# Branch, output and gate/up projections planned by the first stage's list scheduler, with pools opened by phase and shared PSUM

## The chip, the core and the metric

One NeuronCore of a Trainium2 chip runs one decoder layer. The metric is the device time of one execution in microseconds (us). Engines: PE is TensorE (PEld its weight loads), DVE is VectorE, ACT is ScalarE, POOL is GpSimd, SP is the queue that issues most DMAs; ACT issues some DMAs from its own queue. Each engine works through its instructions in the order in which they were recorded, and an instruction that waits holds up all behind it.

## What is computed

```python
S = D_MODEL = 1024; FFN_HIDDEN = 2816
xn = rms_norm(x, norm1_g); proj = xn @ w_in          # q k v | q f i g | two gates
o_sb = stick_breaking_attention(q, k, v)              # 8 heads of 64
o_hg = hgrn2_mixer(...)                               # 4 heads of 128
mixed = sigmoid(gate_sb) * (o_sb @ w_branch[:512]) + sigmoid(gate_hg) * (o_hg @ w_branch[512:])
h = x + mixed @ w_out
hn = rms_norm(h, norm2_g)
out = h + (silu(hn @ w_gate) * (hn @ w_up)) @ w_down
```

All in float32. The matrix products are made of three products of split operands: a value is hi (rounded) plus lo (the rest), and hi·hi + lo·hi + hi·lo are summed in PSUM.

## The kernel before

Everything is transposed (features on partitions, time along the free axis, two halves `h` of 512 columns). It runs in five stages.

1. **First stage** (input projections, attention, HGRN2; all records have line 182, where the plan issues them). `Plan` collects operations with an engine, a duration and a rank; `issue` is a list scheduler that replays them on a model clock and records, on each free engine, the ready operation of highest rank and longest remaining way, once the buffers (`ring`s of a given size) that it needs are free. The gate projections, units `G`, come last; their raw values go to DRAM (`sig_d`) by ACT's queue.
2. **Branch projection** (`pj`, `z` banks; lines 305 to 307): eight blocks `i` of w_branch; attention and HGRN2 outputs are loaded from DRAM (`o_d`) and split. For each block two gates are loaded (`s0`, `s1`), multiplied by the row norm `rr1` on POOL (line 808), put through a sigmoid on ACT (809), and multiplied and added on DVE (816 to 818) into the mixed rows `mx` (hi `ah`, lo `al`).
3. **Output projection** (lines 305 to 307 again, bank `pj`): eight blocks of w_out in the order 0, 4, 1, 5, ..., two halves each. Each result gets x added (862, `xx`), is stored to `h_d` (863, ACT's queue), scaled by the norm's weight (865), squared and summed into `rr` (872, 873), and combined and split into seven Winograd operands `fop` (884 to 889, 848, 849).
4. **Gate/up** (line 919, banks `f`): a Strassen-Winograd form of one level. For each of 11 passes `p`, `left` loads two blocks of w_gate (or w_up) and makes seven split operands (`a_ops`: 902, 903, 905, 910, and 237/238 for the split), and `winograd` makes seven products of 12 matmuls each in three banks x, y, z. After product 1 ACT copies x to `p1` (970 in the first call, 979 later); DVE adds y and p1 after product 6 (976 in the first call, 981 later), before product 7 may go on into the same y bank; further sums are at 986 to 991. A pass is one gate call and one up call, 168 matmuls. `channel_sums` (line 927 on) makes the second norm inside the first call. `down_sums` (945, 955, 958) prepares sums of w_down and writes them to DRAM for stage 5; the results of a pass go to `act_d`.
5. **Down projection** (line 1068), seven products over 11 operand pairs each, accumulated in four banks.

Stages 2 to 5 are written as straight code and put in order by the framework's own scheduler. Stages 1 to 3 have three, two and three PSUM banks called pj, z and ms; stages 4 and 5 rotate through all eight as `f`.

The first `winograd` call is written like this, with `begin` being `channel_sums`:

```python
prod(x, a[1], fop[1], True)
nc.scalar.copy(p1, x)
prod(z, a[5], fop[5], True)
prod(y, a[6], fop[6], True, range(3))
prod(x, a[2], fop[2], False)
prod(y, a[6], fop[6], True, (3,))
begin()
nc.vector.tensor_tensor(c[:, 1], y, p1, op=ALU.add)
prod(y, a[7], fop[7], False)
```

Of the kernel before, what the change touches and what calls it, by code (L numbers as in the profile page):

```python
# [10 lines left out]
F32 = mybir.dt.float32  # L11
# [55 lines left out]
class Buf(View):  # L67
    def __init__(self, ring, make):
        super().__init__(self, lambda t: t)
        self.ring, self.make, self.tile = ring, make, None  # L70
        self.writers, self.readers, self.left, self.held = [], [], 0, False


class Plan:
# [6 lines left out]

    FROM = {"P": 0.2, "D": 2.0}
    TO = {"P": 0.35}

    def __init__(self):
        self.ops, self.caps, self.land = [], {}, {}

# [3 lines left out]
    def op(self, eng, us, calls, rank=0, after=(), part=False, holds=(), lat=None, land=None):  # L91
# [27 lines left out]
        self.ops.append((eng, us, calls, rank, deps, after, bufs, lat))  # L119
        if land:  # L120
            self.land[i] = land
        return i

    def issue(self):
# [18 lines left out]

        way = [0.0] * n
        for i in range(n - 1, -1, -1):
            way[i] = ops[i][1] + max(
                [way[j] + delay(i, j, data) for j, data in succ[i] if ops[j][3] >= 0 or data],
                default=0.0)
        order = lambda i: (-ops[i][3], -way[i], i)
# [9 lines left out]
        while done < n:  # L159
# [6 lines left out]
            for e in engines:  # L166
                while free[e] <= t:
                    for i in ready[e]:
                        need = [b for b in ops[i][6] if b.ring and not b.held]
                        if early[i] <= t and all(  # L170
# [5 lines left out]
                    ready[e].remove(i)  # L176
                    _, us, calls, rank, deps, after, bufs, lat = ops[i]
# [25 lines left out]
def hybrid_block(ctx: ExitStack, tc, xT, wi, wb, wo, wg, wu, wd, vec, outT):  # L203
# [145 lines left out]
    tmpp = st1.enter_context(tc.tile_pool(name="tmpp", bufs=1, reuse_waits="tile"))  # L349
# [12 lines left out]
    where = {tag: (pool, cap) for pool, tags in RINGS.items() for tag, cap in tags.items()}  # L362

    def new(tag, shape=(P, HALF), dt=F32):
        pool, cap = where[tag]
        plan.ring(tag, cap)
        return Buf(tag, lambda: pool.tile(list(shape), dt, tag=tag, bufs=cap, name=tag))
# [4 lines left out]
    def A(fn, *args, n=HALF, aps=0, rank=0, ps=False, part=False, holds=(), **kw):  # L372
        us = (0.05 if ps else 0.093) + n / 1200 + 0.0935 * aps
        return plan.op("A", us, [(fn, args, kw)], rank, part=part, holds=holds)
# [23 lines left out]

    act, tt = nc.scalar.activation, nc.vector.tensor_tensor
    stt, ts = nc.vector.scalar_tensor_tensor, nc.vector.tensor_scalar  # L400

    def rstd(dst, ss, n, rank=0):
        A(act, dst, ss, AF.Ln, ps=True, aps=1, bias=eps_t, scale=1.0 / n, rank=rank)
        A(act, dst, dst, AF.Exp, scale=-0.5, rank=rank)
# [35 lines left out]
    def load(dst, src, kb):  # L440
        last_load[0] = L(dst, src, kb, rank=1, after=(last_load[0],))
# [81 lines left out]
    def take(nm, u, h, ps):  # L523
# [17 lines left out]
        elif nm == "G":  # L541
            x = new("tmp")
            A(nc.scalar.copy, x, ps, ps=True)
            plan.op("A", 0.1, [(nc.scalar.dma_start, (sig_d[u][:, hs(h)], x), {})], lat=2.5)
# [55 lines left out]
    def values(j, last):  # L600
# [12 lines left out]
        for e in range(2):  # L613
            own, oth = slice(64 * e, 64 * e + 64), slice(64 - 64 * e, 128 - 64 * e)
            for sb in range(4):
# [29 lines left out]
                L(o_d[j][own, sb * 256:(sb + 1) * 256], ot[own], 64)  # L645
        return last

    def hgrn(hd, last):
# [5 lines left out]
        for h in range(2):  # L654
# [89 lines left out]
            L(o_d[4 + hd][:, hs(h)], o, 256)  # L744
# [15 lines left out]
    for i, (nm, u) in enumerate(fill):  # L760
# [7 lines left out]
        elif i > 1:  # L768
            w = take_w(COL[nm] + u)
# [6 lines left out]
            if nm == "hg":  # L776
                ends = [f(u, e) for f, e in zip((scores, values, hgrn), ends)]
    with tc.manual_schedule():
        plan.issue()
    c1.close()  # L780
    st1.close()
    st2 = ExitStack()
    op_ = st2.enter_context(tc.tile_pool(name="opool", bufs=1, side="right", reuse_waits="tile"))
    mt = st2.enter_context(tc.tile_pool(name="mt", bufs=2, side="right", reuse_waits="tile"))
    oo = []
    for k in range(KT):
        t = mt.tile([P, S], F32, tag="ld", bufs=4, name="o32")
        nc.sync.dma_start(t, o_d[k])
        hi = op_.tile([P, S], F32R, name=f"oh{k}")
        lo = op_.tile([P, S], F32R, name=f"ol{k}")  # L790
        nc.scalar.copy(hi, t)
        nc.vector.tensor_tensor(lo, t, hi.bitcast(F32), op=ALU.subtract)
        oo.append((hi, lo))
    xst.close()
    mst = ExitStack()
    mx = a_set(mst.enter_context(tc.tile_pool(name="mxp", bufs=1, reuse_waits="tile")))
    wq = [get_w(wb[0])]
    for i in range(KT):
        w = wq.pop(0)
        if i + 1 < KT:  # L800
            wq.append(get_w(wb[i + 1]))
        s0 = mt.tile([P, S], F32, tag="s0", bufs=2, name="s0")
        s1 = mt.tile([P, S], F32, tag="s1", bufs=2, name="s1")
        nc.sync.dma_start(s0, sig_d[i])
        nc.sync.dma_start(s1, sig_d[KT + i])
        for s in (s0, s1):
            for h in range(2):
                nc.gpsimd.tensor_tensor(s[:, hs(h)], s[:, hs(h)], rr1[h], op=ALU.mult)  # L808
            nc.scalar.activation(s, s, AF.Sigmoid)
        for h in range(2):  # L810
            y0, y1 = pj(), pz()
            mm3(y0, w, full[:4], oo, h)
            mm3(y1, w, full[4:], oo, h)
            t0 = mt.tile([P, HALF], F32, tag="t0", name="t0")
            t1 = mt.tile([P, HALF], F32, tag="t1", name="t1")
            nc.vector.tensor_tensor(t0, y0, s0[:, hs(h)], op=ALU.mult)
            nc.vector.tensor_tensor(t1, y1, s1[:, hs(h)], op=ALU.mult)
            nc.vector.tensor_tensor(t0, t0, t1, op=ALU.add)
# [332 lines left out]
```

## Time and profile before

| | us |
|---|---|
| median of 3 runs | 1529.68 (1528.2 to 1530.11) |
| the profiled execution | 1531.17 |
| its span, first to last instruction | 1529.4 |
| PE busy in the span | 1500.8 |

The profile is of one execution; the time around its span is 1531.17 - 1529.4 = 1.77 us. Busy time counts instructions that run, so an engine's idle time is the span less its busy time. In timelines a row has start, duration, engine, line, operation, output and input, and in brackets the idle time before it and what ended that. In rows of waits the numbers are the total, how often, and the longest.

### The profile page before, as it was taken

The page shows a single profiled execution, that of the slowest core. Times are in us where ns is not written, and L with a number is a line of the kernel's source. Part 1 is how long each engine was busy: PE and PEld are TensorE (multiplying, and loading weights), DVE is VectorE, ACT ScalarE, POOL GpSimd, SP SyncE. Part 2 cuts the span into 40 slices and gives each one's busy share as a digit, 9 for nine tenths or more (in the row PEclk, how much of TensorE's full clock was granted, in tenths as well). Part 3 has the DMA queues.
Part 4 walks back from the last instruction along what each step waited for, and adds up shares of the span by engine and source line. Part 5 has one row for each costly group of instructions (what it writes and reads, how often), then busy time and mean ns, then how long its engine had stood idle before and what let it go on. Part 6 is the DMA issues. An engine that isn't in the chain of part 4 may idle for free.

```text
span 1529.4 us, 20448 instructions
## 1 busy us (share of the span) xinstructions
PE 1500.8 (98%) x7213; PEld 1241.2 (81%) x7213; DVE 1179.9 (77%) x2060; ACT 799.1 (52%) x1503; POOL 160.5 (10%) x189
## 2 busy tenths in 40 slices
PE   8999999999999999999999979999999999999999
PEld 6788888888888888888878868888888888878887
DVE  8899779987898777965557789888887777475553
ACT  7866768578858879444333352333333333254442
POOL 4210111111111110114420000000000000000000
PEclk9999999999999999999999999999999999999999
DMA  5111211111111121145434436666633333687672
GB/s 180 42 39 42 83 32 43 47 44 59 41 51 54 59 68 49 52 143 208 139 111 150 140 128 223 221 214 220 221 110 110 111 110 117 245 302 223 191 220 93
DMA packets 78407, 188.53 MB, mean 123 GB/s; under 512 B 9056, under 2 KB 11104, under 8 KB 76896
## 3 DMA queue, kind: packets, MB, share of 16 engines
q1 hardware_dynamic: 68368, 168.34, 33.7%
q10 hardware_dynamic: 9936, 18.88, 3.3%
q8 instruction: 57, 0.93, 0.3%
q14 instruction: 46, 0.38, 0.1%
HBM read 131.61 MB, written 55.57 MB: 122 GB/s over the span
## 4 chain that ended last, share of the span: by engine, by line
PE 72%; DVE 12%; DMA 6%; ACT 4%; issue 4%; POOL 2%; SPq 0%; POOLq 0%; ACTq 0%; DVEq 0%
PE pj L182 24%; PE f L919 20%; PE f L1068 12%; PE ms L182 8%; PE z L182 2%; DMA w<-wu 2%; PE pj L306 2%; PE pj L305 2%; PE pj L307 2%; DVE ol L238 2%; DMA s<-sig_d 1%; ACT aa L182 1%; DMA rb<-act_d 1%; POOL s L808 1%; DMA h_d<-xx 1%
## 5 line engine op out<-in xcount | busy, mean ns | idle before, releaser
L182 PE MATMUL pj<-ah,oh 128*128 128x512 f32 x704 | 286.6, 407 | 1.9 <-POOL oh L182 1.9
L182 PE MATMUL pj<-ah,ol 128*128 128x512 f32 x704 | 276.4, 393 | 1.1 <-DVE ol L182 1.0
L182 PE MATMUL pj<-al,oh 128*128 128x512 f32 x704 | 276.0, 392 | 0.0
L919 PE MATMUL f<-fh,oh 128*128 128x512 f32 x616 | 241.4, 392 | 11.2 <-ACT p L970 7.1
L919 PE MATMUL f<-fl,oh 128*128 128x512 f32 x616 | 240.5, 390 | 0.0
L919 PE MATMUL f<-fh,ol 128*128 128x512 f32 x616 | 240.4, 390 | 0.0
L237 ACT CAST oh<-w 128x512 fp32r<-128x512 f32 x168 | 102.5, 620 | 186.6 <-PE f L919 132.2
L182 PEld LDWEIGHTS pj<-ah,ol 128*128 128x128 f32 x704 | 132.6, 188 | 31.8 <-DVE ol L182 2.4
L182 PEld LDWEIGHTS pj<-ah,oh 128*128 128x128 f32 x704 | 133.0, 189 | 25.4 <-POOL oh L182 2.9
L182 PEld LDWEIGHTS pj<-al,oh 128*128 128x128 f32 x704 | 133.0, 189 | 22.7 <-issue 0.5
L919 PEld LDWEIGHTS f<-fh,oh 128*128 128x128 f32 x616 | 116.1, 189 | 38.4 <-ACT p L970 7.6
L238 DVE TENSOR_TENSOR ol<-w,oh 128x512 fp32r<-128x512 f32 x168 | 115.1, 690 | 35.5 <-ACT oh L237 35.2
L919 PEld LDWEIGHTS f<-fh,ol 128*128 128x128 f32 x616 | 116.1, 188 | 24.5
L919 PEld LDWEIGHTS f<-fl,oh 128*128 128x128 f32 x616 | 116.2, 189 | 23.8
L182 DVE TENSOR_TENSOR_SCAN aa<-aa,ww 128x128 f32<-128x128 f32 (+3 forms) x96 | 92.2, 975 | 33.4 <-ACT aa L182 23.9
L1068 PE MATMUL f<-bh,ah 128*128 128x512 f32 x296 | 114.9, 390 | 1.1 <-ACT acc L1094 1.1
L1068 PE MATMUL f<-bl,ah 128*128 128x512 f32 x296 | 115.4, 390 | 0.5 <-DVE bl L238 0.5
L1068 PE MATMUL f<-bh,al 128*128 128x512 f32 x296 | 115.2, 389 | 0.0
L182 POOL TENSOR_SCALAR oh<-w 128x512 fp32r<-128x512 f32 x84 | 71.1, 846 | 394.2 <-PE pj L182 355.2
L238 DVE TENSOR_TENSOR al<-ra,ah 128x512 fp32r<-128x512 f32 x73 | 50.4, 690 | 76.8 <-ACT ah L237 76.8
L237 ACT CAST ah<-ra 128x512 fp32r<-128x512 f32 x73 | 45.6, 625 | 104.0 <-PE f L1068 92.9
L182 ACT ACTIVATE aa<-aa 128x512 f32<-128x512 f32 (+3 forms) x128 | 69.1, 553 | 4.9 <-DVE aa L182 4.0
(270 smaller groups left out, 2971.2 us busy)
## 6 DMA issues: line engine op xcount, KB each, us to landing
w<-wi SPq DMA_DIRECT2D x42, 512.0 KB, 3.6
rb<-act_d SPq DMA_DIRECT2D x73, 256.0 KB, 4.4
w<-wg SPq DMA_DIRECT2D x22, 512.0 KB, 4.1
w<-wu SPq DMA_DIRECT2D x22, 512.0 KB, 3.7
w<-wd SPq DMA_DIRECT2D x22, 512.0 KB, 7.0
wd_d<-ds SPq DMA_DIRECT2D x44, 256.0 KB, 5.6
ra<-wd_d SPq DMA_DIRECT2D x44, 256.0 KB, 4.1
act_d<-c SPq DMA_DIRECT2D x10, 1024.0 KB, 3.9
```

Source lines behind the costliest of these rows:

```text
L182: fn(*[a.real() if isinstance(a, View) else a for a in args], **{k: v.real() if isinstance(v, View) else v for k, v in kw.items()})
L237: pin(nc.scalar.copy(hi, src))
L238: pin(nc.vector.tensor_tensor(lo, src, hi.bitcast(F32), op=ALU.subtract))
L305: nc.tensor.matmul(out, hi[:, ws], a[ka][0][:, hs(h)], start=first and i == 0, stop=False)
L306: nc.tensor.matmul(out, hi[:, ws], a[ka][1][:, hs(h)], start=False, stop=False)
L307: nc.tensor.matmul(out, lo[:, ws], a[ka][0][:, hs(h)], start=False, stop=last and i == n - 1)
L808: nc.gpsimd.tensor_tensor(s[:, hs(h)], s[:, hs(h)], rr1[h], op=ALU.mult)
L919: nc.tensor.matmul(out, a[i][:, ws], bl[k][j], start=start and k == 0 and i + j == 0, stop=k == 3 and i == 1, skip_group_check=True)
L1068: nc.tensor.matmul(bank[d], l[:, ws], r, start=start and i == 0, stop=p == NP - 1 and i == 2, skip_group_check=True)
```

## The change

Stages 2 to 4 become operations of the same `Plan`, with durations, and one `issue` call records stages 1 to 4. PE's order of matmuls is fixed by a chain (`after=(turn,)`): from the last projection of the first stage on, each group of three waits in the plan for the one before. All other engines take what the list scheduler gives them; stage comes before rank. Pools of later stages are opened when the first of their tiles is recorded, and a tile of phase 2 to 5 is held back in the plan until all operations of the parts named in `BEFORE` are recorded. The gate/up stage uses the banks pj (x), ms (y) and z (z) in rings of 3, 3 and 2 instead of eight `f` banks; `psum2` is opened for stage 5 alone. The gates are multiplied by the row norm on DVE instead of POOL. Results go to `act_d` in eight transfers of 256 KB a pass instead of one of 1024 KB and four of 256 KB. The sum t7 is made in place instead of in a temporary, and all temporaries of stage 3 but one come from the ring `f` of 56. Stages 1 and 5 keep their code.

```diff
+    STAGE = {"s1": 0, "G": 0, "wb": 1, "wo": 1, "ffn": 1}
+    BEFORE = {0: (), 2: ("s1",), 3: ("s1", "G"), 4: ("s1", "G", "wb"), 5: ("s1", "G", "wb", "wo")}
...
-        order = lambda i: (-ops[i][3], -way[i], i)
+        order = lambda i: (stage[i], -ops[i][3], -way[i], i)
...
-                        if early[i] <= t and all(
+                        if early[i] <= t and not any(
+                                left[p] for p in self.BEFORE[phase[i]]) and all(
                                 slots[b.ring] >= sum(c.ring == b.ring for c in need)
                                 for b in need):
...
+    LATER = {
+        ("mt", 2): dict(ld=(4, "ld"), s0=(2, "s0"), s1=(2, "s1"), t0=(2, "t0"), t1=(2, "t1")),
+        ("op", 2): dict(oo=(16, "o")),
+        ("wot", 3): dict(y=(4, "y")),
+        ("mx", 3): dict(mx=(16, "mx")),
+        ("s2p", 4): dict(s2=(2, "s2")),
+        ("fp", 4): dict(f=(56, "f"), rr=(2, "rr")),
+        ("preB", 5): dict(w2=(2, "w"), ds=(4, "ds"), bs=(4, "bs")),
+        ("wA", 5): dict(wA=(2, "w"), ohA=(4, "oh"), olA=(4, "ol")),
+        ("fa", 5): dict(g=(4, "g"), c=(4, "c"), p1=(2, "p1")),
+    }
...
-        for s in (s0, s1):
-            for h in range(2):
-                nc.gpsimd.tensor_tensor(s[:, hs(h)], s[:, hs(h)], rr1[h], op=ALU.mult)
...
+            t = new(ring, (P, S))
+            L(t, sig[j], 512)
+            for h in range(2):
+                V(tt, t[:, hs(h)], t[:, hs(h)], rr[h], op=ALU.mult)
+            A(act, t, t, AF.Sigmoid, n=S + (0 if i or ss else TABLE))
...
-                        t7, t6 = tmp("t7"), blk[0, 0]
-                        nc.vector.tensor_tensor(t7, y, blk[0, 1], op=ALU.subtract)
...
+                    t7, t6 = blk[0, 1], blk[0, 0]
+                    V(tt, t7, y, t7, op=ALU.subtract)
...
+    def prod(out, a, p, start, ks=range(4)):
...
+            turn = plan.op("P", 0.69, [
+                (nc.tensor.matmul, (out, a[p][i][:, ws], fop[p][k][j]),
+                 dict(start=start and k == 0 and i + j == 0, stop=k == 3 and i == 1,
+                      skip_group_check=True)) for i, j in ((0, 0), (0, 1), (1, 0))], after=(turn,))
...
+        x, y, z, p1 = new("pj"), new("ms"), new("z"), new("p1")
+        prod(x, a, 1, True)
+        A(nc.scalar.copy, p1, x, ps=True)
+        if first:
+            prod(z, a, 5, True)
+            prod(x, a, 2, False, (0, 1))
+            prod(y, a, 6, True)
+            channel_sums()
+            V(tt, c[1], y, p1, op=ALU.add)
+            prod(y, a, 7, False)
+            prod(x, a, 2, False, (2, 3))
+        else:
+            prod(y, a, 6, True)
+            V(tt, c[1], y, p1, op=ALU.add)
+            prod(z, a, 5, True)
+            prod(y, a, 7, False)
+            prod(x, a, 2, False)
...
+        for b, t in enumerate((*c, n7, n6, n5, n4)):
+            dst = actd[p][:, b * HALF:(b + 1) * HALF]
+            store_a(dst, t) if p == NP - 1 else L(dst, t, 256, part=True)
...
+    sta.close()
+    preB = pools["preB"]
     psum_st.close()
```

In the recorded order the first stage stays as it was on every engine until its last operations beside the G units, and PE makes the same 6919 matmuls and transposes. The first place where the order differs in weight is ACT's, at the border of the output projection and gate/up. Before (f, yy, t and s are operands of `fop` and of the weight sums, w weights, `parts` the split norm, `p_9238` the copy p1, xx the rows of h):

```order
L863 DMA h_d_152<-xx 128x512
L872 ACTIVATE sq<-xx 128x512
L237 CAST oh<-w_9198 128x512
L927 CAST parts<-rr_8385 128x512
L848 CAST fh<-yy 128x512
L848 CAST fh<-t_9125 128x512
L237 CAST oh<-w_9160 128x512
L848 CAST fh<-yy 128x512
L237 CAST oh<-s_9206 128x512
L848 CAST fh<-yy 128x512
L237 CAST oh<-w_9162 128x512
L970 COPY p_9238<-f 128x512
```

Now, on the same engine at the same place (every planned record has line 194; `bs` is the split norm, y the scaled rows of the last block, `p_9185` the copy p1):

```order
L194 CAST bs<-rr 128x512
L194 CAST oh<-w 128x512
L194 ACTIVATE f<-f 128x512
L194 DMA h_d_152<-f 128x512
L194 CAST f<-y 128x512
L194 COPY p_9185<-pj 128x512
L194 CAST bs<-rr 128x512
L194 CAST oh<-w 128x512
L194 CAST f<-y 128x512 x2
```

The copy p1 stood eight rows behind the split of the norm's second half (`parts<-rr_8385`); it now stands one row ahead of it, behind the square and one cast of the last block.

The second place is DVE's, between the last sum of a pass (z into c) and the first sum of the next gate call (y and p1 into g), at the border of passes 0 and 1. Before:

```order
L991 TENSOR_TENSOR c_9375<-f_9415,c_9375 128x512
L238 TENSOR_TENSOR ol_9546<-w32_9527,oh_9545 128x512
L1013 TENSOR_TENSOR c_9375<-c_9375,g_9197 128x512
L945 TENSOR_TENSOR ds_9982<-w32_9978,ds_9981 128x512
L1016 TENSOR_TENSOR bs_9512<-c_9375 128x512
L238 TENSOR_TENSOR ol_9401<-w32_9376,oh_9400 128x512
L1020 TENSOR_TENSOR bs_9513<-bs_9512,c_9375 128x512
L910 TENSOR_TENSOR w32_9376<-w32_9376,s2_9384 128x512
L1016 TENSOR_TENSOR bs_9514<-c_9375,bs_9513 128x512
L1016 TENSOR_TENSOR bs_9515<-c_9375,bs_9513 128x512
L238 TENSOR_TENSOR ol_9405<-w32_9378,oh_9404 128x512
L981 TENSOR_TENSOR g_9524<-f_9563,p1_9565 128x512
```

Now:

```order
L194 TENSOR_TENSOR c_9412<-z_9405,c_9412 128x512
L194 TENSOR_TENSOR ol_9537<-s2_9509,oh_9529 128x512
L194 TENSOR_TENSOR c_9412<-c_9412,g_9261 128x512
L194 TENSOR_TENSOR c_9501<-c_9501,g_9387 128x512
L194 TENSOR_TENSOR bs_9552<-c_9456,c_9412 128x512
L194 TENSOR_TENSOR ds_9562<-ds_9487,w_9444 128x512
L194 TENSOR_TENSOR ol_9568<-w_9236,oh_9554 128x512
L194 TENSOR_TENSOR bs_9572<-bs_9552,c_9481 128x512
L194 TENSOR_TENSOR ds_9577<-w_9458,ds_9487 128x512
L194 TENSOR_TENSOR g_9585<-ms_9548,p1_9560 128x512
```

Ten instructions stood between the two sums; now eight do, and two of the four `bs` sums follow behind.

The third is DVE's order while PE works on the last G units (o are the split rows of `o_d`, s_7546 the first gate, ol the low halves of weights); before, the two `ol<-w` stood ahead of all `o` rows. Now:

```order
L194 TENSOR_TENSOR o<-ld,o 128x1024 x4
L194 TENSOR_TENSOR s_7546<-s_7546,rr_0_95 128x512
L194 TENSOR_TENSOR s_7546<-s_7546,rr_1_96 128x512
L194 TENSOR_TENSOR ol<-w,oh 128x512
L194 TENSOR_TENSOR o<-ld,o 128x1024
L194 TENSOR_TENSOR ol<-w,oh 128x512
L194 TENSOR_TENSOR s_7600<-s_7600,rr_0_95 128x512
```

The last `ol<-w` is the second half of the last G weight, which PE needs before stage 2; it now stands behind a gate and five rows of `o_d` that come by DMA.

## Rows read from the trace of the kernel before

**Rows 1.** Page, part 1: busy time, share of the span, instructions.
```profile
PE 1500.8 (98%) x7213; PEld 1241.2 (81%) x7213; DVE 1179.9 (77%) x2060; ACT 799.1 (52%) x1503; POOL 160.5 (10%) x189
```
**Rows 2.** Busy time of each engine by stretch; the header names the columns.
```profile
core 0: us, PE busy (x) PEld busy (x) DVE busy (x) ACT busy (x) POOL busy (x), PEclk, DMA share, GB/s
...
673.00:702.00 29.00, 29.00 (x129) 24.00 (x128) 14.45 (x15) 16.14 (x20) 6.22 (x6) 1.00 0.85 306
702.00:790.80 88.80, 87.39 (x385) 72.01 (x385) 52.00 (x73) 32.42 (x45) 38.32 (x29) 1.00 0.36 123
790.80:877.80 87.00, 87.00 (x385) 72.05 (x384) 62.53 (x105) 32.05 (x56) 0.00 (x0) 1.00 0.43 138
877.80:1313.20 435.40, 424.22 (x1853) 348.52 (x1853) 361.64 (x582) 144.67 (x239) 0.00 (x0) 0.99 0.47 160
1313.20:1529.40 216.20, 210.87 (x925) 172.86 (x923) 120.22 (x190) 85.59 (x152) 0.00 (x0) 1.00 0.68 221
```
**Rows 3.** PE's waits: total us, times, longest.
```profile
PE f L919 <- ACT p L970: 7.1, 1, 7.1
PE f L919 <- DVE g L981: 3.0, 5, 0.8
...
PE z L305 <- DVE t L817: 1.4, 1, 1.4
...
PE f L919 <- DVE g L986: 1.0, 1, 1.0
```
**Rows 4.** Timeline of PE, DVE and ACT behind the output projection, each engine by itself.
```profile
885.12 0.39 PE L919 MATMUL f<-fh,ol 128*128 128x512 f32 x1
892.64 0.79 PE L919 MATMUL f<-fh,oh 128*128 128x512 f32 x1 [7.14 <-ACT p L970]
...
885.43 0.69 DVE L884 TENSOR_TENSOR t<-yy 128x512 f32<-128x512 f32 x1 [2.89 <-DMA h_d<-xx]
886.04 0.68 DVE L873 TENSOR_TENSOR rr<-rr,sq 128x512 f32<-128x512 f32 x1
...
886.76 0.62 ACT L927 CAST parts<-rr 128x512 fp32r<-128x512 f32 x1 [3.20 <-DVE rr L873]
...
892.01 0.58 ACT L970 COPY p<-f 128x512 f32<-128x512 f32 x1
```
**Rows 5.** Busy time by stretch, as in Rows 2, just behind that gap.
```profile
892.64:897.10 4.46, 4.46 (x11) 3.49 (x12) 4.46 (x9) 1.14 (x2) 0.00 (x0) 0.50 0.42 118
```
**Rows 6.** PE at the end of the branch projection; POOL's group of gate products.
```profile
786.15 0.39 PE L307 MATMUL pj<-oh,ol 128*128 128x512 f32 x1
787.95 0.50 PE L305 MATMUL z<-oh,oh 128*128 128x512 f32 x1 [1.41 <-DVE t L817]
...
L808 POOL TENSOR_TENSOR s<-s,rr 128x512 f32<-128x512 f32 x32 | 43.3, 1380 | 59.5 <-DMA s<-sig_d 59.5
```
**Rows 7.** DVE around the border of passes 0 and 1; one pass by stretch.
```profile
923.26 0.69 DVE L902 TENSOR_TENSOR w<-w,w 128x512 f32<-128x512 f32 x1 [1.30 <-DMA w<-wu]
...
929.53 0.68 DVE L991 TENSOR_TENSOR c<-f,c 128x512 f32<-128x512 f32 x1
...
936.15 0.68 DVE L981 TENSOR_TENSOR g<-f,p 128x512 f32<-128x512 f32 x1
...
900.00:938.60 38.60, 36.84 (x161) 29.66 (x160) 35.58 (x59) 16.50 (x26) 0.00 (x0) 1.00 0.60 209
```
**Rows 8.** DMA issues: queue, count, KB each, median us from issue to landing.
```profile
w<-wd SPq DMA_DIRECT2D x22, 512.0 KB, 7.0
wd_d<-ds SPq DMA_DIRECT2D x44, 256.0 KB, 5.6
...
h_d<-xx ACTq DMA_DIRECT2D x16, 256.0 KB, 3.5
```
**Rows 9.** ACT's splits of the rows of o_d in the G tail.
```profile
689.88 1.05 ACT L791 CAST oh<-o 128x1024 fp32r<-128x1024 f32 x1 [0.69 <-DMA o<-o_d]
```
**Rows 10.** DVE's last sum of gate/up.
```profile
1313.43 0.69 DVE L991 TENSOR_TENSOR c<-f,c 128x512 f32<-128x512 f32 x1 [1.30 <-PE f L919]
```

More of the change, by code (lines that the diff above doesn't have):

```diff
@@ L361, in hybrid_block @@
     }
[L362 to L367, printed above, removed]
+    where = {tag: (pool, cap, tag, 0) for pool, tags in RINGS.items() for tag, cap in tags.items()}
+    pools, now = {}, [0]
+    st2, fst, mst, sta = ExitStack(), ExitStack(), ExitStack(), ExitStack()
+    LATER = {
[9 more added lines that the diff above has]
+    }
@@ L369, in fixed, with new, make, A @@
+    def new(ring, shape=(P, HALF), dt=F32):
+        pool, cap, tag, phase = where[ring]
+        plan.ring(ring, cap)
+        def make():
+            open_pools(phase)
+            return (pools[pool] if phase else pool).tile(list(shape), dt, tag=tag, bufs=cap, name=tag)
+        return Buf(ring, make, phase)
     def fixed(tile):
         return Buf(None, lambda: tile)
-    def A(fn, *args, n=HALF, aps=0, rank=0, ps=False, part=False, holds=(), **kw):
+    def A(fn, *args, n=HALF, aps=0, rank=0, ps=False, part=False, holds=(), after=(), **kw):
@@ L776, in hybrid_block, with full_split, get_w @@
             if nm == "hg":
+                plan.part = "s1"
                 ends = [f(u, e) for f, e in zip((scores, values, hgrn), ends)]
+    def full_split(src, rings=("oh", "ol"), rank=0):
+        hi, lo = new(rings[0], dt=F32R), new(rings[1], dt=F32R)
+        A(nc.scalar.copy, hi, src, rank=rank)
+        V(tt, lo, src, hi.bitcast(F32), op=ALU.subtract, rank=rank)
+        return hi, lo
+    def get_w(src):
+        t = new("w", (P, 1024))
+        load(t, src, 512, rank=0)
+        return [full_split(t[:, 512 * i:512 * i + 512]) for i in range(2)]
@@ new lines, in hybrid_block, with products @@
+    TABLE = 1536
+    plan.part = "wb"
+    turn = last_fill[0]
+    oo = []
+    for k in range(KT):
+        t = new("ld", (P, S))
+        L(t, od[k], 512)
+        hi, lo = new("oo", (P, S), F32R), new("oo", (P, S), F32R)
+        A(nc.scalar.copy, hi, t, n=S)
+        V(tt, lo, t, hi.bitcast(F32), op=ALU.subtract, n=S)
+        oo.append((hi, lo))
+    def products(out, w, a, ks, h, k0=0, last=True):
+        nonlocal turn
+        for n, k in enumerate(ks):
+            hi, lo = w[(k0 + n) // 4]
+            ws = slice((k0 + n) % 4 * P, ((k0 + n) % 4 + 1) * P)
+            turn = M(1536, [(out, hi[:, ws], a[k][0][:, hs(h)], n == 0, False),
+                            (out, hi[:, ws], a[k][1][:, hs(h)], False, False),
+                            (out, lo[:, ws], a[k][0][:, hs(h)], False, last and n == len(ks) - 1)],
+                     after=(turn,))
@@ L778, in hybrid_block @@
     with tc.manual_schedule():
         plan.issue()
[L780 to L793, printed above, removed]
```

415 lines of the change are left out of this document (201 added, 214 removed).

## The prediction

> **What bounds the kernel now.** I read the page's shares first: PE is busy for 1500.8 of the span of 1529.4 us [rows 1], so the kernel ends when PE has made its products, and a change that adds or removes no product can move the time only through the 28.6 us in which PE stands still, through PE's clock, or by making new idle time. The table by stage says where those 28.6 us lie [rows 2]. While PE works on the last G units it has no gap (29.00 of 29.00); in the branch projection it stands still for 88.80 - 87.39 = 1.41 us, in the output projection not at all, in gate/up for 435.40 - 424.22 = 11.18 us, in the down projection for 216.20 - 210.87 = 5.33 us. The rest lies in the first stage. The first stage keeps its order and the last keeps its code, so what the change can win is in the 12.6 us of the middle.
>
> The waits name them [rows 3]: one of 7.1 us for ACT's copy p1, five of about 0.6 us (3.0) for DVE's sum that frees the y bank, one of 1.0 us for a sum of z, and one of 1.4 us in the branch projection for DVE's t. Together 12.5 us. The reader should also see what is not there: no wait for a weight and none for x. PE's pace where nothing stops it is the output projection's 87.00 / 385 = 0.226 us a matmul [rows 2].
>
> A wait costs a little more than the row names. In the branch projection the matmul before starts at 786.15 and the next at 787.95 [rows 6]: 1.80 - 0.226 = 1.57 us where 1.41 are named, 0.16 more. Eight such waits make 1.3 us. The long one costs something else too. Behind it, PE ran at a granted clock of 0.50, the level of 1.2 GHz, and eleven matmuls took 4.46 us [rows 5]; at 0.226 they take 2.49, so 1.97 us were lost. PE had stood still for 7.14 us just before [rows 4]. All that this stretch of the program can give back is 12.5 + 1.3 + 1.97 = **15.8 us**.
>
> **The change, part by part.**
>
> *The border of output projection and gate/up.* PE stopped because ACT had not copied x into p1 (892.01) [rows 4]. Followed back: ACT's copy stood eight rows behind `parts<-rr`, which started at 886.76 after a wait of 3.20 us for DVE's addition into rr (886.04). That addition was late because the instruction ahead of it on DVE, t7, had itself waited 2.89 us for a store of xx to `h_d` to land. t7 is a new temporary in a ring of seven, and the ring's oldest tile was still being stored. So a store held DVE, DVE held ACT, ACT held PE. The change makes t7 in place, which takes away the store's wait, and puts p1 ahead of the second `parts` row and of the casts. Either alone would shorten the chain. I count the whole wait as gone: 7.1 + 0.16 + 1.97 = 9.2 us.
>
> What is late next there? DVE. Between PE's last product of the output projection and the first sum of y and p1 it has the last xx sum and fifteen more instructions. One takes 0.61 us from start to start where DVE does not wait (885.43 to 886.04) [rows 4], so the y sum starts 16 × 0.61 = 9.8 us after the projection's end and ends 0.69 later, at about 10.5. PE makes 12 + 12 + 6 + 12 + 4 matmuls first, 46 × 0.226 = 10.4 us. The two are level, and DVE's hand-overs with ACT can only delay it. I charge **1.2 us** (0 if none delays it; 4.6, half the old gap, if several do).
>
> *Between passes.* The five short waits come in the first passes, where DVE is busy for 35.58 of 38.60 us and itself waits for weights (1.30) [rows 7]. From the last sum of one call (929.53) to the first y sum of the next (936.15) DVE needed 6.6 us for eleven steps, while PE makes only two products in that time, 24 × 0.226 = 5.4. In the new order eight instructions stand between the two sums, nine steps, 9 × 0.61 = 5.5 us. That is almost exactly PE's 5.4, so the waits become small, not certainly zero. I take back all of the 3.0 and 1.0 and charge **1.2 us** for what remains (0 to 4, all of them).
>
> *Branch projection.* POOL's 32 gate products took 1380 ns each [rows 6] and go away. PE's one wait there was for DVE's t. DVE takes over 32 × 0.69 = 22 us, by the length of one such product [rows 7], in a stage where it is busy for 52.00 of 88.80 us [rows 2]; 74 of 88.8 leaves it free one sixth of the time, and that free time is what hides the products. Without that cover the 22 us would be PE's. The wait of 1.41 I count as gone.
>
> *G tail.* Here the new order makes something later. The low half of the last G weight now stands behind a gate, which comes by DMA, and five rows of `o_d`, of which before's fifth was cast only at 689.88 after a wait for its load [rows 9]. The cast ends at 690.9, DVE follows with its own row and a few instructions of 0.6 to 1.1 us, so the half is there at about 694. PE's last 32 or so matmuls before 702 begin close to that. **0.5 us** (0 to 3: three DVE instructions late).
>
> *Hand-over to the last stage.* The last sum of z starts at 1313.43 and ends 0.69 later [rows 10]; the stage begins at 1313.20. With three shared banks instead of eight, its early products may meet the bank that this sum reads: 1314.12 - 1313.20 = 0.9 us, less what PE makes meanwhile in other banks. **0.5 us** (0 to 1.5).
>
> *Transfers.* `act_d` goes out in eight transfers of 256 KB instead of five, on SP's queue, three more issues a pass, with weight loads behind them. SP waits in order, so a load could start later; PE waits for no weight in before's rows [rows 3], and the DMA engines are busy for 0.47 of gate/up [rows 2]. I charge nothing, because a weight's sums come a whole call ahead of its product; without that cover each late load would be DVE's stall, and that is one of the rivals.
>
> Sum: -15.8 + 1.2 + 1.2 + 0.5 + 0.5 = **-12.4 us**. Against the profiled execution that is 1531.17 - 12.4 = 1518.8; the median of the runs lies 1.49 below that execution, so **1517.3**. With all charges at their low ends it is 1531.17 - 15.8 - 1.49 = 1513.9, with all at their high ends (13.1) 1527.0.
>
> **The rivals.** *The chain gets shorter but does not go.* DVE's sixteen steps or ACT's casts replace the store, and half of the border's 9.2 us stays: 1517.3 + 4.6 = 1521.9. For it: DVE and PE are level to 0.1 us in my own count. Against it: the store, the first cause, is really gone.
>
> *DVE stalls for w_down (slower).* The plan packs the sums of w_down for all eleven passes into about the first five, where DVE has 38.60 - 35.58 = 3.0 us to spare a pass, 15 us in five [rows 7]. It counts 512 / 350 + 2.0 = 3.5 us for a load, 4.9 for the second of a pair; the trace has 7.0 from issue to landing, and 5.6 for the stores that free their ring [rows 8]. If each group stands at the head of DVE's queue when the plan thought its load had landed, DVE stalls there for 2.1 to 3.5 us with PE's next y sum behind it. Eleven times that is 23 to 38 us, less the 15 to spare: 8 to 23 us of new idle time on PE, a time of 1525 to 1540. It decides from 2.5 us of stall a group on, where 11 × 2.5 - 15 eats the 12.4. For it: the plan's figure is below the measured one. Against it: these sums have the lowest rank, so the plan uses them to fill holes well after the landing; before, they ran in about as few passes, with waits of 0.6 us on PE.
>
> *The shared banks cost at each border of calls.* 22 calls now take x, y and z from rings of three, three and two. If PE had to wait at each of the 21 borders for the sum that ends a call, 0.9 + 0.16 us as above, it would be 21 × 1.06 = 22 us, a time of 1517.3 + 22 = 1539. Against it: rings of two or three leave a whole call, 84 × 0.226 = 19 us, for that sum, and the repeated short waits of before are for a reader of the very bank that PE is in, which more banks would not help [rows 3]. The Trainium skill (Perfetto Trace Analysis, section Optimization Strategy) says that the same gap repeating on the engine that should be saturated can mean that there is not enough SBUF or PSUM for the next tile. By that rule before's five equal gaps would call for more banks, and the change, which has no more than eight, would be the wrong way; the row's named releaser, DVE's g, says otherwise.
>
> *The edit does nothing.* That t7's wait, p1's place and the gates' engine all change leaves little room for it; a time within 3 us of before would need new waits to eat the gain, and so belongs to the stalls for w_down.
>
> **How the numbers follow.** My forecast, 1517.3, has 0.68; the shorter chain 0.12; the stalls for w_down 0.16, of which 0.06 end near before's time; the banks 0.04. A measurement of this kernel can tell about 0.2%, 3.1 us, from no change. Faster: 0.68 + 0.12 = 0.80. Same 0.06. Slower 0.10 + 0.04 = 0.14. The range goes from the sum's low end to its high end, 1513.5 to 1527.5, which takes in the shorter chain and leaves out the other two, 0.20.
>
> **What the new profile would show.** Right: no wait of several us behind the output projection, t7 without a wait for `h_d`, p1 copied within a microsecond of product 1, no stretch at clock 0.50 there; PE's waits for y sums below 2.5 us in the first call and below 1.2 in all later ones; DVE busy for about 74 us in the branch projection with PE at its 0.226; gate/up near 427 us instead of 435.4, and the last G units within half a microsecond of 29. Wrong: DVE waits for `w<-wd` or for `wd_d` stores of over 2 us each with y sums behind, PE waits that repeat at every border of calls for a sum of z, or a gap ahead of stage 2 for the low half of the last G weight.

## The result and the profile after

The changed kernel takes 1532.82 us (median of 12 runs) where the kernel before takes 1529.62 beside it: a ratio of 1.0022 [1.0014, 1.0029]. It is slower by about 3 us; 1517.3 was forecast. One run of 5328.1 us is left out of the ratio; without it the median is 1532.55.

The profiled execution took 1530.12 us, which is one of the fastest of the twelve, and its span is 1528.4. A second profile of the same kernel, taken with the experiments, has a span of 1531.8. Both are read here, because the difference between them lies in the places that turned out to matter.

The page's busy times of the changed kernel, to be held against [rows 1]:

```profile
PE 1501.5 (98%) x7213; PEld 1241.6 (81%) x7213; DVE 1191.4 (78%) x2092; ACT 800.8 (52%) x1503; POOL 115.5 (8%) x157
```

Busy time by stretch, the stages as in [rows 2] (G tail, branch projection, output projection, gate/up, down projection):

```profile
673.00:702.29 29.29, 28.89 (x127) 23.58 (x126) 17.41 (x20) 17.68 (x22) 1.39 (x2) 1.00 0.87 305
702.29:789.33 87.04, 87.04 (x385) 72.08 (x384) 65.38 (x104) 33.38 (x45) 0.00 (x0) 1.00 0.36 124
789.33:876.37 87.04, 87.04 (x385) 72.08 (x384) 61.73 (x102) 34.68 (x58) 0.00 (x0) 1.00 0.41 136
876.37:1308.71 432.34, 423.27 (x1853) 346.73 (x1852) 357.43 (x578) 140.86 (x236) 0.00 (x0) 1.00 0.48 160
1308.71:1528.40 219.69, 212.56 (x925) 173.88 (x923) 120.75 (x190) 86.12 (x152) 0.00 (x0) 0.99 0.67 220
```

The two projections run without a gap, and gate/up starts at 876.37 instead of 877.86. But gate/up is only 3.0 us shorter than before's 435.4, and the down projection is 3.5 us longer than its 216.2. PE's waits say where, in the rows that answer to [rows 3] and in the down projection's:

```profile
PE z L194 <- DVE ol L194: 5.6, 6, 1.8
...
PE f L1136 <- ACT acc L1162: 2.7, 1, 2.7
PE ms L194 <- DVE g L194: 2.1, 3, 1.5
...
PE z L194 <- ACT oh L194: 1.4, 1, 1.4
```

The 7.1 us for the copy p1 are gone, and so are before's waits for DVE's t. New are six waits for the low half of a weight sum that a product into z needs (`ol`), and one for a high half. DVE's own waits between 900 and 1070 us lead further:

```profile
DVE ds L194 <- DMA w<-wd: 7.5, 7, 2.4
DVE w L194 <- DMA w<-wu: 4.1, 3, 1.9
DVE ol L194 <- ACT oh L194: 3.8, 4, 1.7
DVE w L194 <- DMA w<-wg: 2.2, 3, 1.3
```

In the kernel before, DVE did not wait for `w<-wd` at all in this stretch, and 4.2 us for `w<-wu`. The timeline of DVE and PE around the second pass shows one such chain:

```profile
927.71 0.69 DVE L194 TENSOR_TENSOR ds<-w 128x512 f32<-128x512 f32 x1 [1.39 <-DMA w<-wd]
...
931.49 0.69 DVE L194 TENSOR_TENSOR ds<-ds,w 128x512 f32<-128x512 f32 x1 [0.34 <-DMA wd_d<-ds]
...
938.32 0.69 DVE L194 TENSOR_TENSOR w<-w 128x512 f32<-128x512 f32 x1 [0.55 <-DMA w<-wg]
...
944.55 0.50 PE L194 MATMUL z<-f,ol 128*128 128x512 f32 x1 [1.72 <-DVE ol L194]
```

Three transfers hold DVE for 1.39 + 0.34 + 0.55 = 2.28 us in all, it works on with hardly a pause behind each, and PE loses 0.44 us at a y sum (931.20) and 1.72 us at the next weight sum.

In the down projection the row of ACT's copy `acc` answers to a wait of 1.1 us before. Before's ACT:

```profile
1343.34 0.62 ACT L237 CAST ah<-ra 128x512 fp32r<-128x512 f32 x1 [2.51 <-PE f L1068]
1343.87 0.61 ACT L237 CAST bh<-rb 128x512 fp32r<-128x512 f32 x1
1344.39 0.61 ACT L237 CAST ah<-ra 128x512 fp32r<-128x512 f32 x1
1344.91 0.58 ACT L1094 COPY acc<-f 128x512 f32<-128x512 f32 x1
```

and the changed kernel's at the same place:

```profile
1339.04 0.62 ACT L249 CAST ah<-ra 128x512 fp32r<-128x512 f32 x1 [2.13 <-DMA ra<-wd]
1339.57 0.62 ACT L249 CAST bh<-rb 128x512 fp32r<-128x512 f32 x1
...
1341.13 0.61 ACT L249 CAST ah<-ra 128x512 fp32r<-128x512 f32 x1
1341.65 0.61 ACT L249 CAST bh<-rb 128x512 fp32r<-128x512 f32 x1
1342.17 0.61 ACT L249 CAST ah<-ra 128x512 fp32r<-128x512 f32 x1
1342.69 0.57 ACT L1162 COPY acc<-f 128x512 f32<-128x512 f32 x1
```

Before, three casts stand between ACT's last issue of an `hb` load and the first copy; now seven do. The stage's code is the same, but its order is made by the framework's scheduler, and that order moved. Four casts are 4 × 0.52 = 2.1 us, and the wait grew by 2.74 - 1.07 = 1.7. Behind it the granted clock fell, as the stretches of 10 us of the changed kernel show (the last three columns are clock, DMA share and GB/s):

```profile
1338.71:1348.71 10.00, 7.26 (x26) 5.41 (x25) 9.02 (x15) 9.25 (x18) 0.00 (x0) 0.83 1.05 384
1348.71:1358.71 10.00, 10.00 (x46) 8.29 (x45) 9.80 (x18) 3.68 (x8) 0.00 (x0) 1.00 0.84 272
```

26 matmuls took 7.26 us; at 0.226 each they take 5.9, so 1.4 us went with the clock. Another 0.3 went with the bank at the hand-over, where two matmuls start 0.50 us apart (1309.16 and 1309.66). With the 1.7 of the wait that is 3.4 of the 3.5 us.

### The profile page after: what moved, and what is told of

The parts are those of the page before. It is cut to its first block, busy times and chain, and to the rows that moved or that the text cites. A ratio compares the mean times of both kernels' runs of the same rounds, so it can differ in the third digit from the quotient of the medians.

```text
span 1528.4 us, 20496 instructions
## 1 busy us (share of the span) xinstructions
PE 1501.5 (98%) x7213; PEld 1241.6 (81%) x7213; DVE 1191.4 (78%) x2092; ACT 800.8 (52%) x1503; POOL 115.5 (8%) x157
## 4 chain that ended last, share of the span: by engine, by line
PE 76%; DVE 11%; DMA 5%; ACT 4%; issue 3%; POOL 0%; SPq 0%; DVEq 0%; ACTq 0%; POOLq 0%
PE pj L194 37%; PE ms L194 17%; PE f L1136 12%; PE z L194 11%; DVE ol L194 2%; DMA w<-wd 1%; ACT aa L194 1%; DMA rb<-act_d 1%; DVE g L194 1%; DVE c L194 1%; DVE aa L194 1%; DVE tail L194 1%; DMA w<-wu 1%; DVE ds L194 1%; DMA ld<-o_d 1%
## 5 line engine op out<-in xcount | busy, mean ns | idle before, releaser
L194 DVE TENSOR_TENSOR ol<-w,oh 128x512 fp32r<-128x512 f32 x248 | 171.3, 691 | 40.8 <-ACT oh L194 34.5
L194 PE MATMUL ms<-f,oh 128*128 128x512 f32 x528 | 163.2, 390 | 2.1 <-DVE g L194 2.1
L194 PEld LDWEIGHTS pj<-ah,ol 128*128 128x128 f32 x704 | 132.8, 189 | 31.9 <-DVE ol L194 2.5
L194 PEld LDWEIGHTS ms<-f,oh 128*128 128x128 f32 x528 | 98.7, 188 | 24.5 <-DVE g L194 3.4
L194 PE MATMUL z<-f,oh 128*128 128x512 f32 x352 | 108.6, 390 | 1.4 <-ACT oh L194 1.4
L194 PE MATMUL pj<-f,oh 128*128 128x512 f32 x352 | 108.4, 389 | 0.0
L194 PE MATMUL ms<-f,ol 128*128 128x512 f32 x264 | 102.8, 389 | 0.0
L194 PE MATMUL pj<-mx,oh 128*128 128x512 f32 x256 | 78.8, 389 | 0.0
L194 PEld LDWEIGHTS z<-f,oh 128*128 128x128 f32 x352 | 66.0, 188 | 15.3 <-ACT oh L194 1.8
```

The source lines that it names most:

```text
L194: fn(*[a.real() if isinstance(a, View) else a for a in args], **{k: v.real() if isinstance(v, View) else v for k, v in kw.items()})
```

## The experiments

The theories were: (1) DVE stands at the head of its queue for w_down transfers that the plan believes landed, and transfers crowd one another; (2) DVE's new order, or the number of its instructions in the first passes, is late by itself; (3) the down projection takes back what gate/up wins. Each run was timed beside the kernel before. "Gate/up" and "down" are lengths in us in its profile, "waits" PE's waits in gate/up. The profile is of one execution, the median of several: before's profile lies 1.5 us above its median, those of after, spread and nowait 2.7, 3.0 and 2.4 us below theirs.

| run | median us | ratio to before | gate/up | waits | down |
|---|---|---|---|---|---|
| before | 1529.6 | 1 | 435.4 | 11.1 | 216.2 |
| after | 1532.8 | 1.0022 [1.0014, 1.0029] | 432.3 | 9.1 | 219.7 |
| after_again | 1533.2 | 1.0022 [1.0013, 1.0032] | 434.2 | 10.5 | 221.8 |
| land | 1531.0 | 1.0013 [1.0003, 1.0022] | 431.2 | 7.6 | 222.1 |
| spread | 1520.8 | 0.9942 [0.9927, 0.9956] | 421.6 | 0.5 | 218.0 |
| b_t7 | 1526.7 | 0.9981 [0.9969, 0.9992] | 429.8 | 7.4 | 217.5 |
| pool_ds | 1557.5 | 1.0178 [1.0164, 1.0192] | 459.5 | 26.1 | 219.9 |
| spread2 | 1533.5 | 1.0026 [1.0017, 1.0035] | 434.8 | 10.0 | 221.1 |
| latehb | 1535.3 | 1.0037 [1.0023, 1.0050] | 433.9 | 9.1 | 221.6 |
| spread_latehb | 1521.8 | 0.9947 [0.9935, 0.9960] | 421.3 | 0.4 | 222.3 |
| nowait | 1528.1 | 0.9990 [0.9981, 0.9998] | 429.1 | 5.2 | 218.9 |
| acc8 | 1528.1 | 0.9991 [0.9982, 1.0000] | 434.6 | 9.3 | 215.8 |
| spread_acc8 | 1516.0 | 0.9912 [0.9898, 0.9926] | 421.9 | 0.8 | 216.2 |
| all3 | 1513.3 | 0.9893 [0.9878, 0.9907] | 421.5 | 0.6 | 213.6 |
| small | 1518.2 | 0.9937 [0.9926, 0.9949] | 420.7 | 0.2 | 219.4 |
| b_acc8 | 1528.2 | 1.0000 [0.9992, 1.0008] | 433.4 | 9.7 | 214.8 |
| b_three | 1520.5 | 0.9949 [0.9937, 0.9961] | 429.2 | 6.9 | 213.4 |

**after_again**, no edit. 

> The changed kernel itself, for a second profile beside the one in which it took 1530.12 us, 2.7 less than its median of 1532.82. Theory 1 (the time is lost where DVE waits for transfers, and transfers vary): a profile near the median has the same nine or ten us of waits in gate/up, and the extra two or three us lie in gate/up while w_down is loaded, or in the first 60 us of the down projection. Theory 2 (the new order itself is late): the waits of PE stand at the same places with the same lengths to 0.3 us, and the profiles differ elsewhere or not at all. Median 1532 to 1534, 3 us above before.

 The profiled execution took 1533.5 us. Against the first profile gate/up is 1.8 us longer and the down projection 2.1 us: both places, as theory 1 has it.

**land.**

```diff
-            last_wd[0] = L(t, r, 512, after=(last_wd[0],))
+            last_wd[0] = L(t, r, 512, after=(last_wd[0],), land=5.0)
```

> The plan counts 5.0 us instead of 2.0 from the end of a w_down load's transfer to its use, nothing else. Theory 1 (DVE stands at the head of its queue for w_down loads that the plan believed landed): DVE's 7.5 us of waits for w<-wd fall below 2, PE's waits for ol in front of z (5.6 us, six) fall below 2.5, and the time is 3 to 6 us below the changed kernel's. Theory 2 (DVE's order of sums and splits is late whatever the loads do): PE's waits for ol stay above 4 us in all, time within 1.5 us of the changed kernel.

 DVE's waits for `w<-wd` vanished, but those for the other weights rose, between 880 and 1310 us from the changed kernel's 4.1 and 2.3 to these:

```profile
DVE w L194 <- DMA w<-wu: 10.4, 5, 3.3
DVE w L194 <- DMA w<-wg: 6.8, 5, 2.0
```

PE's waits for `ol` stayed at 5.4 us. A better figure for one transfer only handed the lateness to the next; the time came out near theory 2's, by a mechanism of theory 1.

**spread.**

```diff
-            last_wd[0] = L(t, r, 512, after=(last_wd[0],))
+            last_wd[0] = L(t, r, 512, after=(last_wd[0], turn))
```

> The sums of w_down of pass p are loaded only after the gate call of pass p, so one group a pass instead of eleven in five passes. Theory 1: no wait of DVE for w<-wd in gate/up, DVE has more than 5 us to spare in each pass, PE's waits in gate/up fall from 9.2 to below 2 us, time 6 to 9 us below the changed kernel (1524 to 1527), unless the down projection gives it back. Theory 2: PE's waits for ol remain in each pass. A third theory (what is won early is lost again where the first product of the down projection waits for its transfers): gate/up is 7 us shorter, the down projection 4 or more longer, and the time is not under 1529.

 Better than expected, 12.0 us below the changed kernel. PE's waits of gate/up in its profile are these, and there are no others:

```profile
PE ms L194 <- DVE c L194: 0.3, 1, 0.3
PE ms L194 <- DVE g L194: 0.2, 1, 0.2
```

Theory 3 is not borne out in the form that was stated: the down projection took 218.0 us, 1.8 more than before, and kept its wait of 2.7 us for acc, this time with the clock at 1.00 behind it. This is an execution 3.0 us below the run's median, so in others the loss there may be larger.

**b_t7**, the kernel before with the one edit.

```diff
-                        t7, t6 = tmp("t7"), blk[0, 0]
-                        nc.vector.tensor_tensor(t7, y, blk[0, 1], op=ALU.subtract)
+                        t7, t6 = blk[0, 1], blk[0, 0]
+                        nc.vector.tensor_tensor(t7, y, t7, op=ALU.subtract)
```

> The kernel before with one edit: t7 is made in place instead of in a temporary whose oldest tile is still being stored. If that store was the first cause of the 7.1 us at the border, DVE's wait of 2.9 us for h_d goes, the gap shrinks to 2 to 5 us, the clock behind it may stay high, and the time is 3 to 6 us below before. If the order of ACT's casts ahead of the copy p1 was enough by itself, the gap stays above 6 us and the time is within 1 us of before.

 It gained 2.9 us by the ratio. Its border is

```profile
887.05 0.50 PE L919 MATMUL f<-fh,oh 128*128 128x512 f32 x1 [1.30 <-ACT p L970]
893.75 0.50 PE L919 MATMUL f<-fh,oh 128*128 128x512 f32 x1 [0.91 <-DVE g L976]
```

so 7.1 us became 2.2 in two waits, and the clock stayed at 1.00. The edit also let the scheduler move products of the first call, so not all of it is the store's. In b_acc8 below, whose border is the old one, DVE's wait for the store was 1.2 us instead of 2.9 and PE's gap 5.5 instead of 7.1: 1.7 less here, 1.6 less there.

**pool_ds.** The sums of w_down on POOL:

```diff
-        V(tt, s7, a11, a21, op=ALU.subtract)
+        G(nc.gpsimd.tensor_tensor, s7, a11, a21, op=ALU.subtract, us=1.38)
...
```

> The sums of w_down are made on POOL instead of DVE, as densely packed as in the changed kernel; DVE has 44 instructions less in its first passes and none that waits for w<-wd. If what delays PE is DVE standing or working for these sums, PE's waits in gate/up fall from 9.2 to below 3 us and the time to 1524 to 1528. If it is the transfers themselves that crowd out the weights of gate/up (as far as the delayed plan hints, where DVE's waits moved to w<-wu and w<-wg, 17 us), DVE's waits for w<-wu and w<-wg are above 8 us, PE's waits above 5, and the time is above 1529.

 28 us slower than before, by a cause outside both theories. DVE's group of weight splits between 952 and 990 us, in the changed kernel and then in this one:

```profile
L194 DVE TENSOR_TENSOR ol<-w,oh 128x512 fp32r<-128x512 f32 x11 | 7.5, 681 | 0.0
```

```profile
L194 DVE TENSOR_TENSOR ol<-w,oh 128x512 fp32r<-128x512 f32 x9 | 11.9, 1330 | 0.0
```

An instruction of 681 ns takes 1330 while POOL adds. DVE's splits are slowed to half by the engine that was to relieve it. The Trainium skill (Perfetto Trace Analysis, section Optimizing Scalar/DVE Operations) says that the two share a read port of SBUF and that moving work between them might not help; the trace agrees, with these two means. The run tells nothing about the theories.

**spread2.** The edit of spread, and two groups a pass instead of one, each behind one call:

```diff
-        down_sums(p)
+        if 2 * p < NP:
+            down_sums(2 * p)
...
         x, c = winograd(au, "c")
+        if 2 * p + 1 < NP:
+            down_sums(2 * p + 1)
```

> One group of w_down sums for each winograd call, so two a pass, between the changed kernel's three or so and the one a pass of the spread version; this is about the density of the kernel before. If density decides, PE's waits in gate/up lie between 0.5 and 9 us, at 2 to 4 us, time 1523 to 1526. If it is only that the plan's loads are believed early, two groups placed behind a call's end still wait as before: PE's waits above 6 us and the time above 1528.

 No gain at all: DVE waits 4.6 us for `w<-wd` again and PE 10.0 us, now for y sums (c 6.5, g 3.5). Half of the packing away is not half of the loss. The kernel before has this density too, and 4 us of short waits; the DMA share between 914 and 1104 us is 0.59 to 0.67 here and 0.64 to 0.67 there. So density alone does not decide. The numbers are those of the second outcome, but loads that are believed early are not all of it. One of the four waits for c:

```profile
972.57 0.69 DVE L194 TENSOR_TENSOR w<-w 128x512 f32<-128x512 f32 x1 [0.68 <-DMA w<-wg]
...
983.59 0.68 DVE L194 TENSOR_TENSOR c<-ms,p 128x512 f32<-128x512 f32 x1
...
984.32 0.73 PE L194 MATMUL ms<-f,oh 128*128 128x512 f32 x2 [1.45 <-DVE c L194]
```

Between the first two rows DVE works without a gap, with two w_down sums among the rest, and no wait for `w<-wd` stands there. In this order DVE's own row of work is late too. Why two groups a pass cost PE 10.0 us and one group 0.5 was not taken apart.

**latehb.**

```diff
-            if o == 1 and p >= 3:
-                for k, h in HB[2 * p - 6:2 * p - 4]:
+            if o in DOWN[1:3]:
+                n = p + NP * (o == DOWN[2])
+                for k, h in HB[n:n + 1]:
```

> The changed kernel, with the sixteen loads of h (4 MB) taken out of the first product of the down projection and put into the second and third. If the transfers of that product make ACT's copies into acc late, PE's wait of 2.7 to 3.3 us for acc falls below 1, the clock stays at 1.00 behind it, the down projection takes 214 to 217 us instead of 219.7 to 221.8, and the time is 1527 to 1530. If ACT's own order (splits ahead of the copies) is the reason, the wait stays above 2 us and the time within 1.5 us of the changed kernel.

 The opposite: the wait for acc grew to 5.8 us, the clock fell to 0.68 over 10 us, and the time rose 2.5 us. The edit did not do what it was meant to. The framework's scheduler put fifteen of the sixteen loads of h ahead of the first copy into acc all the same, and closer to it: seven casts stood between the last of them and that copy, now there is one. ACT's rows there:

```profile
1338.13 4.41 ACTq L1156 DMA_DIRECT2D hb<-h_d  x3
1342.65 0.62 ACT L249 CAST ah<-ra 128x512 fp32r<-128x512 f32 x1 [3.92 <-DMA hb<-h_d]
...
1344.20 0.98 ACTq L1156 DMA_DIRECT2D hb<-h_d  x2
1345.30 0.62 ACT L249 CAST ah<-ra 128x512 fp32r<-128x512 f32 x1 [1.51 <-DMA rb<-act_d]
1345.82 1.06 ACT L1163 COPY acc<-f 128x512 f32<-128x512 f32 x2
```

PE came to the end of the first product 1.4 us sooner after its start (30.5 us instead of 31.9), but the first copy came 1.7 us later (35.7 instead of 34.0), behind loads that ACT was still issuing. So the run does not tell what loads behind the copies would do. **spread_latehb**, the same with the edit of spread: 

> Both edits, one group of w_down sums a pass and the loads of h later. If the two losses are separate they add: 8 to 9 us in gate/up and 3 to 4 in the down projection, 1516 to 1520. If the second only moves transfers that are needed anyway, it equals the spread version, 1520 to 1522.

 1521.8, and again all of PE's loss in the first product gathered in one wait:

```profile
PE f L1136 <- ACT acc L1163: 7.0, 1, 7.0
```

**acc8.** The second product of the down projection in four banks of its own:

```diff
-        first = o in (1, 6, 5)
+        first = o in (1, 2, 6, 5)
...
-        if o in (6, 7, 4):
+        if o in (2, 6, 7, 4):
```

> The changed kernel with the second product of the down projection in four banks of its own, so that it need not wait until ACT has copied the first product out (four more additions on DVE later). If that wait and the clock's fall behind it are what makes the down projection 3.5 to 5.6 us longer than before's 216.2, the down projection falls to 213 to 217 us and the time to 1527 to 1530. If the transfers of that stretch bound it, PE waits as long for a split or a load a little later, and the time stays within 1.5 us of the changed kernel.

 The wait for acc is gone, the clock stays at 1.00, the down projection takes 215.8 us: 3.9 to 6.0 less than in the two profiles of the changed kernel, and the median is 4.7 lower, while gate/up is no better. **spread_acc8** 

> One group of w_down sums a pass and the second product in banks of its own. If gate/up and the down projection lose separately, the spread version's 1520.8 falls by its 2.7 us for acc to 1517 to 1519. If transfers bound the start of the down projection, 1520 to 1522.

 and **all3**, with latehb too, 

> The same with the loads of h later as well, where PE's whole loss in the first product had gathered in one wait for acc (7.0 us). If the copies to acc were the reason of that wait, 1513 to 1516; if the transfers were, the 7 us come back as waits for splits of the second product and the time is 1519 to 1522.

 show that the losses are separate: 1516.0 and 1513.3. The 7 us did not come back in another place. Beside the medians, all3's lengths are these (gate/up, down):

```profile
876.40:1297.76 421.36, 420.77 (x1853) 347.27 (x1852) 359.05 (x578) 141.63 (x236) 0.00 (x0) 1.00 0.48 164
1297.76:1511.40 213.64, 209.92 (x925) 173.16 (x923) 123.12 (x194) 87.37 (x152) 0.00 (x0) 1.00 0.69 226
```

**nowait.** Order and transfers as they are; the four sums read an operand that has long been in SBUF.

```diff
+        e = fop[1][0][0].bitcast(F32)
+        for j, (o, x, y, op) in enumerate(((s7, e, e, ALU.subtract), (s6, e, s7, ALU.subtract),
+                                           (s5, s6, e, ALU.add), (s3, e, s6, ALU.subtract))):
+            r = plan.ops[n0 + j]
+            plan.ops[n0 + j] = (*r[:2], [(tt, (o, x, y), dict(op=op))], *r[3:])
```

> The changed kernel with the same order and the same transfers, but the four w_down sums of a pass read an operand that has been in SBUF for long (their values, and so the last stage's, are other ones), so DVE never waits for w<-wd. If these waits at the head of DVE's queue (7.5 to 9.1 us) are what delays PE in gate/up, PE's waits there fall from 9 or 10 us to below 4 and the time to 1525 to 1529. If it is the number of DVE's instructions in the first passes, or the transfers that crowd out w<-wu and w<-wg, PE's waits stay above 6 us and the time within 2 us of the changed kernel.

 PE's waits fell to 5.2 us and the median by 4.7: between the two outcomes. Standing for w_down is a part of the loss. **small** takes the transfers away as well (a w_down load or store of 32 columns):

```diff
+            plan.ops[last_wd[0]] = (*q[:2], [(nc.sync.dma_start, (t[:, :32], r[:, :32]), {})], *q[3:])
...
+            plan.ops[n1] = (*q[:2], [(nc.sync.dma_start, (wdd[p][:, b * HALF:b * HALF + 32], t[:, :32]), {})], *q[3:])
```

> As the version in which the w_down sums read an operand that is in SBUF, and besides each of their loads and stores moves only 32 of 1024 or 512 columns (the last stage reads w_down itself, and other values come out), so the order stays and 22 MB of transfers go from the first passes. It tells apart what is left of PE's waits in gate/up when DVE no longer waits for w<-wd (5.2 us). If it is the transfers, which bring w<-wu, w<-wg and the stores late, PE's waits fall below 2 us and the time to 1522 to 1526. If it is the number of DVE's instructions in the first passes, they stay above 4 us and the time within 1.5 us of that version's 1528.

 PE's waits fell to 0.2 us though DVE did every one of its instructions in the same order:

```profile
952.00:990.00 38.00, 38.00 (x170) 31.45 (x169) 36.97 (x61) 12.23 (x21) 0.00 (x0) 1.00 0.36 106
```

DVE is busy for 36.97 of 38 us here and PE for all of them. So theory 2 falls for the changed kernel: its order and its number of instructions are fine without these transfers, and the whole of gate/up's loss is in them, partly where DVE stands for w_down and partly where w_down's traffic brings other weights and stores late. By PE's waits (9.1, then 5.2, then 0.2) the two parts are about equal; by the medians (1532.8, 1528.1, 1518.2) the first is a third.

**b_acc8**, acc8's edit in the kernel before: 

> The kernel before with the second down product in banks of its own. Before's wait for acc was 1.1 us with no fall of the clock. If the loss in the down projection came with the change, before gains 0.5 to 1.5 us. If before loses as much there in most executions as the changed kernel does, it gains 3 to 5 us, as that one did.

 No change; before did not lose by this wait what the changed kernel lost. **b_three**, the kernel before with the edits of b_t7, acc8 and latehb: 

> The kernel before with t7 in place, the second down product in banks of its own and the loads of h later: all that the experiments found outside the plan. If the plan's order of gate/up (once its w_down sums are spread) is worth what its profile says, this stays 5 to 8 us above the 1513.3 of the best version, 1519 to 1522. If the same few edits do it without the plan, it comes within 3 us of it.

 1520.5. The plan with spread sums is worth 7 us more than that (1513.3), nearly all of it in gate/up, 429.2 against 421.5. How much of the 7 us the spreading would bring without the plan was not run.

## Why the prediction was wrong

*Border of output projection and gate/up*: right. PE's one wait there is 0.2 us, p1 is copied at 879.32, less than a microsecond after its product, and the clock stays at 1.00: the 9.2 us were gained. The charge of 1.2 for the first y sum was too much by 1.0.

*Branch projection*: right, PE has no gap. DVE took 65.38 us, not 74, since part of its other work grew cheaper without POOL beside it (last section). *G tail*: charged 0.5, measured 0.40, for the very `ol` named. *Hand-over*: charged 0.5; the bank cost 0.3.

*Transfers*: the first step that failed. "I charge nothing, because a weight's sums come a whole call ahead of its product" holds where DVE has time to spare and the transfers do too. The 44 w_down sums start between 888.3 and 1045.2 us instead of between 895.7 and 1093.2, so their 22 MB went in 157 us instead of 197. DMA's share is the last but one column of a stretch of the changed kernel, and then of the kernel before:

```profile
990.00:1028.00 38.00, 34.74 (x150) 27.47 (x148) 32.31 (x54) 10.77 (x19) 0.00 (x0) 1.00 0.84 282
```

```profile
990.00:1028.00 38.00, 37.34 (x165) 30.57 (x164) 33.42 (x55) 11.42 (x20) 0.00 (x0) 1.00 0.65 222
```

There the weights' sums were late. I had counted both kernels' packing as about five passes. The packing is not the whole cause, since spread2, with a DMA share like before's, lost 10.0 us too; what is shown is that the loss goes when w_down's transfers go (small) or come one group a pass (spread). The rival that I put at 0.16 was the right mechanism, mis-sized: DVE's stalls for w_down were 7.5 us, not 23 to 38, but other weights' loads added to them, and PE paid mostly at the low halves of weights (5.6 us), less at the y sums that I watched (2.1). In the sum: -9.2 for the border, and the other waits went from 4.0 to 9.1 us instead of to the charge of 1.2; with 0.16 for each of the four more waits that is -9.2 + 5.1 + 0.6 = -3.5, measured -3.0.

*"The last keeps its code, so what the change can win is in the 12.6 us of the middle"*: the second step that failed. The last stage kept its code and not its order: ACT's copies of acc moved behind four more casts. That cost 3.5 us in the first profile and 5.6 in the second; acc8 gives it back.

Together: -1.5 (up to the first product of gate/up) - 3.0 + 3.5 = -1.0 us of span in the first profile, and -2.0 - 1.2 + 5.6 = +2.4 in the second, which is nearer the median's +3.2. The third rival, banks short at each border of calls, is excluded: no wait for a z sum of the call before is in the rows, and spread leaves PE 0.5 us of waits with the same rings. By the rule of the Trainium skill that went with it (Perfetto Trace Analysis, section Optimization Strategy), gaps that repeat can mean too few buffers; here the repeating gaps had DVE as releaser before and went with the transfers after.

With the two losses taken out, 1513.3 us is 16.3 below before; of that, 2.6 us (213.6 against 216.2) are the down projection's own.

## What to carry to other kernels

A list schedule that gives low rank to transfer-fed work packs it as early as its modelled landings allow; if an in-order engine stands near its limit there, pace that work by the critical engine's progress, and thinly, rather than by a better landing figure: one group a pass brought 12.0 us, two a pass nothing. When code ahead of a scheduled stage changes, read that stage's new order too, not only its code: a copy that frees a bank may have moved. When an edit moves loads, read from the trace where they ended up in their queue: fifteen of sixteen still stood ahead of the copy that PE wanted, and they helped only once that copy no longer held PE.

## What the runs showed of the hardware

DVE's splits `ol<-w,oh` on 128x512, with both operands in SBUF, took 681 ns without POOL and 1330 ns beside POOL's additions (means of 1560 to 1699 ns there, pool_ds). The branch projection shows a milder form of it: the sum of two gate products took 1036 ns before, with POOL at work, and 689 after. Instructions with one operand in PSUM were not slowed: in the branch projection before, six `t<-pj,s` and six `t<-z,s` lay beside POOL's gate products for over 80% of their length and took 683 and 685 ns. And a wait of much the same length did not always cost the clock: behind 2.7 us the granted clock fell to 0.83 over 10 us in the changed kernel and stayed at 1.00 in spread and nowait (2.7 and 2.8 us). What decided that is open.
